# Attention queries kept once in fp32 and split on the chip before use, instead of stored and loaded as two parts

## The chip, the cores and the metric

One NeuronCore of a Trainium2 chip runs the whole program. The metric is the device time of one execution in microseconds (us); lower is better. Engines are named as the profile names them: PE (matrix multiply; PEld its weight loads), DVE (vector), ACT (scalar and activation), POOL and SP (here mainly issuers of DMAs).

## The reference

One layer of a hybrid encoder: a modulated RMSNorm, one input projection, a 2-D neighbourhood attention beside a bidirectional mLSTM, and one output projection with a residual and a final RMSNorm. Sequence 2048 (a grid of 32 rows by 64 columns), model width 1024, 8 attention heads of 64, all in fp32.

```python
proj = h @ w_in + b_in                       # (2048, 4624)
# attention: each token looks at 8 grid rows x 16 grid columns around it
qg = to_grid(q) * (NA_HEAD_DIM ** -0.5)
s = einsum('bhrcd,bhrjkd->bhrcjk', qg, kg) + bias[None]
s = where(col_mask[:, None, :], s, -inf)
p = softmax(s.reshape(..., kh * GRID_W), axis=-1)
o = einsum('bhrcjk,bhrjkd->bhrcd', p, vg)
na_out = o * silu(na_z)
# beside it: ml_out from a chunkwise bidirectional mLSTM
y = concatenate([na_out, ml_out], axis=-1) @ w_out
out = rmsnorm(x + gate * y)
```

## The kernel before

Products that need full accuracy are made as three fast passes: each operand is a high part (rounded to the fast matrix format, fp32r) and a low part (the rest), and high x high, low x high and high x low are summed in PSUM.

The program runs in stages. From 0 to about 520 us the norm, the token-side projections and the convolutions are made. Then `nq_gen` makes the remaining projections tile by tile as a generator (one `yield` per matmul, line 986), and `pump(n)` lets it run n matmuls between the steps of the mLSTM passes, so that PE always has something to do. For attention queries (kind `q`, 16 tiles of 128 channels x 512 tokens) ACT writes the high part from PSUM (line 1020), DVE the low part (line 1021), and both are stored to the DRAM scratch `d_qna`; the stores wait in the list `late` and are issued on ACT's queue a few matmuls later (line 989).

From about 960 us on, `phase2` runs the attention. The 16 patches of 128 queries have four units each (a unit is two heads), and two units are a pair. `slot(m)` works on pair m, and there are 32 slots with new scores. In a slot PE does, in this order: the 12 score matmuls of pair m (`scores`, line 1477, tile pS), the value matmuls of pair m-1 (line 1520, tile pO), a few matmuls of the output projection as filling (`pump`, line 1565, tile y), and then four times the transposes of one head's weights (`turned`, line 1505, tile pT), each followed by filling: 6, 5, 5, 4 and 4 matmuls in a steady slot, 8, 7, 7, 7 and 7 in the first three. The last four filling matmuls stand right before the scores of the next slot. DVE adds the bias table and takes the minimum (line 1485), ACT exponentiates (line 1486), DVE normalises (line 1497), and ACT copies each transposed tile out of PSUM (line 1507, tile pt). In every second slot, `mixed` also splits the patch's mixed heads for the output projection (ACT line 1535, DVE line 1540), while DVE adds finished output tiles to x (line 1570) and ACT squares them (line 1572).

The score matmuls of one unit take the query as their stationary operand, in pairs of heads: high query x high key, low query x high key, high query x low key. `load_q(m+2)`, at the start of slot m, loads a pair's queries, both parts at once, into one of three buffers `qs`; the first two go through POOL, the third through ACT, the others through SP. In slots 2 and 3 `split_w` splits the output weights (ACT line 1457, DVE line 1458, 128x1024 each).

Inside `manual_schedule` the instructions of an engine stand as the code emits them; outside, a scheduler places them. Everything from slot 0 on is emitted inside it; the end of the mLSTM before slot 0 is not.

Of the kernel before, what the change touches and what calls it, by code (L numbers as in the profile page):

```python
# [8 lines left out]
F32 = mybir.dt.float32  # L9
F32R = mybir.dt.float32r  # L10
AF = mybir.ActivationFunctionType
ALU = mybir.AluOpType
# [3 lines left out]
P = 128  # L16
# [4 lines left out]
GT = 512  # L21
# [41 lines left out]
class Kernel:  # L63
# [30 lines left out]
    def scratch(self):  # L94
        d = self.dram
        self.d_vna = d.tile([T, 512], F32, name="d_vna")
        self.d_ck = d.tile([MH, NC, P, 897], F32, name="d_ck")
        self.d_mneg = d.tile([P, CH], F32, name="d_mneg")
        self.d_zna = d.tile([16, P, 4, P], F32, name="d_zna")
        self.d_zml = d.tile([16, P, 4, P], F32, name="d_zml")  # L100
        self.d_qna = d.tile([2, 2, 16, P, 2, P], F32, name="d_qna")
        self.d_kna = d.tile([2, 512, T], F32, name="d_kna")
        self.d_mix = d.tile([16, P, 4, P], F32, name="d_mix")
        self.d_wo = d.tile([KT, P, D], F32, name="d_wo")
        self.d_fnw = d.tile([1, D], F32, name="d_fnw")
        self.d_gate = d.tile([1, D], F32, name="d_gate")
        self.d_rneg = d.tile([NH, 15, 31], F32, name="d_rneg")
        nks = [24, 32, 24]
        self.d_e = [d.tile([NH, 16, 15, nks[t]], F32, name=f"d_e{t}") for t in range(3)]
        nrs = [11, 15, 12]  # L110
        self.d_t = [[d.tile([NH, P, nrs[r] * nks[t]], F32, name=f"d_t{r}{t}") for t in range(3)] for r in range(3)]
# [853 lines left out]
    def nq_gen(self):  # L965
        nc = self.nc
        whi, wlo = self.wslot[0]
        both, upper, lower = range(NG), (3, 2), (1, 0)
        turns = [(s, both) for s in (0, 1, 2, 3)] + [(s, upper) for s in (4, 5, 6, 7, 8, 9, 10, 11, 12, 14, 13, 15)]
        turns += [(s, lower) for s in (8, 9, 10, 11, 4, 5, 6, 7)]  # L970
        turns += [(15, (1, 0)), (14, (1, 0)), (13, (1,)), (12, (1, 0)), (13, (0,))]
        order = [(i, s, g) for i, (s, gs) in enumerate(turns) for g in gs]
        needs = [i for i, (s, gs) in enumerate(turns) if i == 1 or i > 1 and s != turns[i - 2][0]]
        raw = self.nq_load(needs[0], turns[needs[0]][0])
        late, parity = [], False
        for i, s, g in order:
            off = (i % 2) * P
            kind, ct = ("mz", "nz", "k", "q")[s // 4], s % 4
            patch = kind != "k"
            col = {"mz": 20, "nz": 8, "k": 4, "q": 0}[kind] + ct  # L980
            bias = self.bcol[:, col : col + 1]
            ps = self.pp.tile([P, GT], F32, tag="pp", name=f"pq_{s}_{g}")
            for k in range(KT):
                w1, w2 = whi[:, k, off : off + P], wlo[:, k, off : off + P]
                for n, (w, h) in enumerate(((w1, self.hhi), (w1, self.hlo), (w2, self.hhi))):
                    self.mark = nc.tensor.matmul(patch_ps(ps) if patch else ps, w, self.htok(h, g, k, patch), start=(k == 0 and n == 0), stop=(k == KT - 1 and n == 2))  # L986
                    if k == 2 and n == 0:
                        while late:
                            nc.scalar.dma_start(*late.pop(0))
                    if i == len(turns) - 1 and k % 2 and n == 2:  # L990
                        self.lastload(k // 2)
                    if k == 2 and n == 0:
                        if needs and needs[0] == i + 1:
                            needs.pop(0)
                            self.nq_split(*raw)
                            if needs:
                                raw = self.nq_load(needs[0], turns[needs[0]][0])
                    if k < KT - 1 or n < 2:
                        yield
            if kind == "k" and g in lower:  # L1000

                hv, lv = (self.kk[ct][:, e * T + g * GT : e * T + (g + 1) * GT] for e in range(2))
                nc.scalar.activation(hv, ps, AF.Identity, bias=bias)
                nc.vector.scalar_tensor_tensor(lv, ps, bias, hv.bitcast(F32), ALU.add, ALU.subtract)
                yield
                continue
            parity = not parity
            if parity:
                both = self.qst.tile([P, 1032], F32R, tag="st", name=f"qst_{s}_{g}")
            else:  # L1010
                both = self.raw.tile([P, 1024], F32R, tag="raw1", name=f"qst_{s}_{g}")
            hv, lv = both[:, 0:512], both[:, 512:1024]
            if kind in ("mz", "nz"):
                hv = hv.bitcast(F32)
                nc.scalar.activation(hv, ps, AF.Silu, bias=bias)
                dst = (self.d_zna if kind == "nz" else self.d_zml)[4 * g : 4 * g + 4, :, ct].rearrange("a p q -> p a q")
                nc.scalar.dma_start(dst, hv.rearrange("p (a q) -> p a q", a=4))
                self.zdone.add((kind, ct, g))
            else:
                nc.scalar.activation(hv, ps, AF.Identity, bias=bias)  # L1020
                nc.vector.scalar_tensor_tensor(lv, ps, bias, hv.bitcast(F32), ALU.add, ALU.subtract)
                for e, part in enumerate((hv, lv)):
                    src = part.bitcast(F32).rearrange("p (a q) -> p a q", a=4)
                    if kind == "q":
                        dst = self.d_qna[e, ct // 2, 4 * g : 4 * g + 4, :, ct % 2].rearrange("a p q -> p a q")
                    else:
                        dst = self.d_kna[e, ct * P : (ct + 1) * P, g * GT : (g + 1) * GT].rearrange("p (a q) -> p a q", a=4)
                    late.append((dst, src))
            if (s, g) in ((15, 3), (15, 2)):
                self.freed.append(g)  # L1030
            yield
        while late:
            nc.scalar.dma_start(*late.pop(0))
# [308 lines left out]
    def phase2(self):  # L1342
        nc = self.nc
# [44 lines left out]
        def load_q(i):  # L1388
            if 2 * i >= NU:
                return  # L1390
            b, c0 = units[2 * i][0], min(units[2 * i][1], units[2 * i + 1][1])
            (nc.gpsimd, nc.gpsimd, nc.scalar, nc.sync)[min(i, 3)].dma_start(qs[i % 3].bitcast(F32), self.d_qna[:, c0 // 2, b].rearrange("e p c q -> p e c q"))

        def load_v(b, most=4, queue=nc.gpsimd):

# [285 lines left out]
        def slot(m):  # L1681
            new = (2 * m, 2 * m + 1) if 2 * m < NU else ()
            old = (2 * m - 2, 2 * m - 1) if m else ()
            if m:
                load_q(m + 2)
            if new:
                scores(new)
            if old:
                po = values(old)
            if new:  # L1690
                normalised(new[0])
            if old:
                gated(old, po)
            if new:
                normalised(new[1])
            b = units[old[0]][0] if m > 2 and old[0] % 4 == 2 else None
            if not new:
                mixed(b, 1)
                mixed(b, 0)
                for _ in range(2):  # L1700
                    self.pump(12)
                    finish()
                    step()
                return
            fills = [8, 7, 7, 7, 7] if m < 3 else [6, 5, 5, 4, 4]
            for n in range(-1, 4):
                if n >= 0:
                    turned(new[n // 2], n % 2)
                    if n % 2:
                        step()  # L1710
                    finish()
                    if n in (1, 2) and b is not None:
                        mixed(b, n % 2)
                    if n in (0, 2):
                        loads(new[n // 2])
                    if n == 1 and self.reloads:
                        self.reloads.pop(0)()
                for fn in extra.pop((m, n), ()):
                    fn()
                self.pump(fills[n + 1])  # L1720
            if m == 2:
                self.pump(max(0, self.left) + 1)
                self.owed = 0
                mixed(b0, 1)
                mixed(b0, 0)

        with self.tc.manual_schedule():
            for m in range(NU // 2 + 1):
                slot(m)
            while len(done) < len(patches):  # L1730
# [85 lines left out]
```

## Time and profile before

| | |
|---|---|
| median of 3 runs | 1331.33 us (1327.65 to 1332.96) |
| profiled execution, its own time | 1328.63 us |
| its span | 1326.9 us |
| PE busy | 1294.6 us, 98% |
| DVE, ACT, POOL busy | 779.6 us (59%), 542.8 us (41%), 225.1 us (17%) |
| DMA | 255.91 MB, mean 193 GB/s |

The span runs from the first to the last instruction of the program; the execution's own time has 1.7 us around it. A row of the timeline has start, duration, engine, line, operation and tiles, and in brackets how long the engine was idle before and who ended it. Names such as hhi, hlo, whi_a are those of buffers that are used again: in the score matmuls `hhi` and `hlo` hold attention keys, in the output projection the weights.

### The profile page before, as it was taken

To read this page: it belongs to the slowest core of one execution; us is meant where nothing else is said; L and a number is where in the kernel's file an instruction comes from. 1 tells how busy PE (TensorE), PEld (TensorE's weight loads), DVE (VectorE), ACT (ScalarE), POOL (GpSimd) and SP (SyncE) were. 2 spreads that over 40 slices of the span, in tenths; PEclk is the share of its full clock that TensorE was granted. 3 is DMA by queue.
4 is the path that set the end of the run, shared out by engine and by line. 5 is a ranking of instruction groups with operands and counts; after the bars stand their busy time and mean duration, and the time that the engine had idled before them with its cause. 6 is when DMAs were issued, how large, how long until landed. Compare 5 with 4: busy or idle time off the path is not lost. (4 is left out here: it accounts for less than half of the span.)

```text
span 1326.9 us, 23404 instructions
## 1 busy us (share of the span) xinstructions
PE 1294.6 (98%) x8330; PEld 1115.4 (84%) x8330; DVE 779.6 (59%) x2406; ACT 542.8 (41%) x1184; POOL 225.1 (17%) x280
## 2 busy tenths in 40 slices
PE   9999999999999999999999999999999999999996
PEld 8899999999878787888888888888777778778785
DVE  5754452112455559176768878767547576666663
ACT  5643324543222323123324323333356555565551
POOL 0243103331000000012212002121202211212211
PEclk9999999999999999999999999999999999999999
DMA  9998657998267685545756866746689977868871
GB/s 325 323 281 180 169 141 171 214 244 217 82 149 208 142 209 165 159 120 167 204 165 196 254 187 204 237 141 188 198 256 239 212 184 190 195 175 194 195 186 48
DMA packets 240487, 255.91 MB, mean 193 GB/s; under 512 B 31079, under 2 KB 200295, under 8 KB 240371
## 3 DMA queue, kind: packets, MB, share of 16 engines
q1 hardware_dynamic: 157006, 182.98, 50.7%
q0 software_dynamic: 20496, 36.21, 11.2%
q10 hardware_dynamic: 62868, 35.22, 9.6%
q8 instruction: 66, 1.08, 0.4%
q14 instruction: 51, 0.41, 0.1%
HBM read 169.81 MB, written 92.72 MB: 198 GB/s over the span
## 5 line engine op out<-in xcount | busy, mean ns | idle before, releaser
L986 PE MATMUL pq<-hhi,whi_a 128*128 128x512 f32 x512 | 208.2, 407 | 0.8 <-ACT u L891 0.8
L986 PE MATMUL pq<-hlo,whi_a 128*128 128x512 f32 x512 | 208.4, 407 | 0.0
L986 PE MATMUL pq<-hhi,wlo_a 128*128 128x512 f32 x512 | 206.7, 404 | 0.0
L986 PEld LDWEIGHTS pq<-hhi,whi_a 128*128 128x128 f32 x512 | 96.8, 189 | 17.8 <-ACT u L891 1.3
L986 PEld LDWEIGHTS pq<-hhi,wlo_a 128*128 128x128 f32 x512 | 96.8, 189 | 16.3
L986 PEld LDWEIGHTS pq<-hlo,whi_a 128*128 128x128 f32 x512 | 96.7, 189 | 16.0 <-issue 0.5
L1507 ACT ACTIVATE pt<-pT 96x384 f32<-96x384 f32 (+3 forms) x128 | 65.8, 514 | 86.7 <-PE pT L1505 84.0
L1486 ACT ACTIVATE pbuf<-pbuf,mn 128x480 f32<-128x480 f32 (+5 forms) x128 | 76.0, 594 | 53.0 <-DVE mn L1485 53.0
L960 POOL TENSOR_TENSOR wlo_a<-rawq,whi_a 128x1024 fp32r<-128x1024 f32 x19 | 45.8, 2409 | 296.1 <-ACT whi_a L959 263.7
L1565 PE MATMUL y<-hhi,whi_a 128*128 128x512 f32 x256 | 91.4, 419 | 0.5 <-ACT whi_a L1535 0.5
L1565 PE MATMUL y<-hhi,wlo_a 128*128 128x512 f32 (+1 forms) x272 | 90.7, 399 | 0.2 <-ACT y L1572 0.2
L1485 DVE CUSTOM_DVE_ANT_0 pbuf<-pS,tab 128x480 f32<-128x480 f32 (+5 forms) x128 | 62.9, 540 | 39.1 <-PE pS L1477 32.1
L1230 ACT ACTIVATE num<-px,gtile 128x129 f32<-128x129 f32 x120 | 38.3, 366 | 111.3 <-PE px L1225 86.5
L1505 PEld LDWEIGHTS pT<-ident,pbuf 128*128 128x128 f32 (+2 forms) x416 | 51.0, 137 | 29.6 <-issue 9.9
L618 DVE TENSOR_TENSOR stvo<-pvo,brow 128x256 f32<-128x256 f32 x64 | 26.6, 422 | 83.1 <-PE pvo L548 65.7
L1505 PE MATMUL pT<-ident,pbuf 128*128 128x128 f32 (+2 forms) x416 | 67.3, 275 | 8.2 <-DVE pbuf L1497 6.8
L546 PE MATMUL pvo<-whi_b,hhi 128*128 128x256 f32 x256 | 72.6, 284 | 0.0
L548 PE MATMUL pvo<-whi_b,hlo 128*128 128x256 f32 x256 | 72.1, 281 | 0.0
L547 PE MATMUL pvo<-wlo_b,hhi 128*128 128x256 f32 x256 | 72.0, 281 | 0.0
L1249 POOL TENSOR_TENSOR hm<-hm,ck 128x128 f32<-128x128 f32 x64 | 26.5, 414 | 252.9 <-DVE hm L1248 223.9
L833 ACT ACTIVATE dec<-dec,gtile 128x128 f32<-128x128 f32 x128 | 42.7, 393 | 53.6 <-POOL dec L826 50.8
L581 DVE TENSOR_TENSOR stv<-pv,brow 128x256 f32<-128x256 f32 x32 | 12.4, 421 | 74.4 <-DMA d_vna<-stv 43.4
(302 smaller groups left out, 3408.3 us busy)
## 6 DMA issues: line engine op xcount, KB each, us to landing
ck<-d_ck SPq DMA_DIRECT2D x64, 384.5 KB
rawq<-in_w_main_dram SPq DMA_DIRECT2D x28, 512.0 KB
raw<-in_w_main_dram SPq DMA_DIRECT2D x20, 512.0 KB
d_ck<-stvo SPq DMA_DIRECT2D x16, 514.0 KB
kv<-d_ck SPq DMA_DIRECT2D x64, 128.5 KB
wada<-in_w_ada_dram SPq DMA_DIRECT2D x32, 256.0 KB
dec<-d_mneg SPq DMA_DIRECT2D x32, 256.0 KB
d_ck<-dec ACTq DMA_DIRECT2D x32, 256.0 KB
```

Source lines behind the costliest of these rows:

```text
L546: nc.tensor.matmul(ps, lhi(k), rhi(k), start=(k == 0), stop=False)
L547: nc.tensor.matmul(ps, lhi(k), rlo(k), start=False, stop=False)
L548: self.mark = nc.tensor.matmul(ps, llo(k), rhi(k), start=False, stop=(k == KT - 1))
L833: nc.scalar.activation(t[:, o, :], t[:, o, :], AF.Exp, bias=self.cols["g"][:, d, h, c : c + 1])
L960: (eng or nc.gpsimd).tensor_tensor(lo[:, :, cs], raw, hi[:, :, cs].bitcast(F32), ALU.subtract)
L986: self.mark = nc.tensor.matmul(patch_ps(ps) if patch else ps, w, self.htok(h, g, k, patch), start=(k == 0 and n == 0), stop=(k == KT - 1 a ...
L1230: nc.scalar.activation(num[:, d, :], px[:, d, :], AF.Copy, scale=self.cols["inter"][:, d, h, c : c + 1])
L1485: nc.vector.tensor_tensor_reduce(pt[:, :nk], ps, tabs[place[u]][j][:, :nk], 1.0, 3e38, ALU.add, ALU.min, mn)
L1486: nc.scalar.activation(pt[:, :nk], pt[:, :nk], AF.Exp, bias=mn, scale=-1.0, accum_out=sums[:, j : j + 1])
L1505: nc.tensor.transpose(ps[:cs, i, :], U[u][j][:, i * cs : (i + 1) * cs], self.ident)
L1507: nc.scalar.activation(t[:cs, :nch, :], ps[:cs, :nch, :], AF.Copy)
L1565: nc.tensor.matmul(y, m[:, k, :], w[k][:, cs], start=(k == 4 and n == 0), stop=(k == 3 and n == 2))
```

## The change

Queries are stored once, in fp32: ACT alone evicts the tile, and one store leaves instead of two. `load_q` loads that single copy into the low half of the buffer. The new `split_q(i)` makes the parts on the chip: ACT copies the loaded values, rounded, into the high half, and DVE subtracts the high half from the low half in place. `slot(m)` calls `split_q(m + 1)` after its fourth transposes and before its last four filling matmuls; `split_q(0)` is called before slot 0.

```diff
-        self.d_qna = d.tile([2, 2, 16, P, 2, P], F32, name="d_qna")
+        self.d_qna = d.tile([2, 16, P, 2, P], F32, name="d_qna")
...
+            elif kind == "q":
+                hv = hv.bitcast(F32)
+                nc.scalar.activation(hv, ps, AF.Identity, bias=bias)
+                dst = self.d_qna[ct // 2, 4 * g : 4 * g + 4, :, ct % 2].rearrange("a p q -> p a q")
+                late.append((dst, hv.rearrange("p (a q) -> p a q", a=4)))
             else:
                 nc.scalar.activation(hv, ps, AF.Identity, bias=bias)
                 nc.vector.scalar_tensor_tensor(lv, ps, bias, hv.bitcast(F32), ALU.add, ALU.subtract)
...
-            (nc.gpsimd, nc.gpsimd, nc.scalar, nc.sync)[min(i, 3)].dma_start(qs[i % 3].bitcast(F32), self.d_qna[:, c0 // 2, b].rearrange("e p c q -> p e c q"))
+            (nc.gpsimd, nc.gpsimd, nc.scalar, nc.sync)[min(i, 3)].dma_start(qs[i % 3][:, 1].bitcast(F32), self.d_qna[c0 // 2, b])
+
+        def split_q(i):
+            if 2 * i < NU:
+                hi, lo = qs[i % 3][:, 0], qs[i % 3][:, 1]
+                nc.scalar.activation(hi, lo.bitcast(F32), AF.Copy)
+                nc.vector.tensor_tensor(lo, lo.bitcast(F32), hi.bitcast(F32), ALU.subtract)
...
+                if n == 3:
+                    split_q(m + 1)
                 self.pump(fills[n + 1])
...
         with self.tc.manual_schedule():
+            split_q(0)
             for m in range(NU // 2 + 1):
                 slot(m)
```

The order of ACT's instructions at the end of slot 18 and the start of slot 19, a slot with mixing, before (pt is the copy of a transposed tile, y the square, pbuf the exponential of the next slot's scores):

```order
L1572 ACTIVATE y_0_12389,fss_12387<-xr_12428 128x512
L1535 ACTIVATE whi_a<-zs 128x512
L1507 ACTIVATE pt_1_12568<-pT_1_12563 128x512
L1486 ACTIVATE pbuf_10151,sums_12592<-pbuf_10151,mn_0_12593 128x480
L1486 ACTIVATE pbuf_10152,sums_12592<-pbuf_10152,mn_1_12596 128x480
```

and in the changed kernel:

```order
L1580 ACTIVATE y_0_12393,fss_12391<-xr_12432 128x512
L1543 ACTIVATE whi_a<-zs 128x512
L1515 ACTIVATE pt_1_12574<-pT_1_12569 128x512
L1399 ACTIVATE qs_10029<-qs_10029 128x256
L1494 ACTIVATE pbuf_10133,sums_12600<-pbuf_10133,mn_0_12601 128x480
```

The high part of slot 19's queries is made behind the last copy of slot 18's transposed tiles, and nothing else moved. DVE at the same place, before (whi_a is the low part of the mixed heads, xr the sum with x):

```order
L1540 TENSOR_TENSOR whi_a<-whi_a 128x512
L1570 TENSOR_TENSOR xr_12428<-xr_12428,y_0_12389 128x512
L1540 TENSOR_TENSOR whi_a<-zs,whi_a 128x512
L1570 TENSOR_TENSOR xr_12428<-xr_12428,y_1_12431 128x512
L1485 ISA pbuf_10151,mn_0_12593<-pS_0_12576,tab_10051 128x480
```

and in the changed kernel:

```order
L1548 TENSOR_TENSOR whi_a<-whi_a 128x512
L1578 TENSOR_TENSOR xr_12432<-xr_12432,y_0_12393 128x512
L1548 TENSOR_TENSOR whi_a<-zs,whi_a 128x512
L1400 TENSOR_TENSOR qs_10029<-qs_10029 128x256
L1578 TENSOR_TENSOR xr_12432<-xr_12432,y_1_12435 128x512
L1493 ISA pbuf_10133,mn_0_12601<-pS_0_12584,tab_10035 128x480
```

The low part stands behind the mixed heads' low part. The third place is DVE before slot 0, outside the hand-written order, where the last mLSTM group is normalised (an iterated root, nwt and rstd, then mu). In the changed kernel:

```order
L1339 TENSOR_TENSOR nwt_3_10012<-rstd_3_10009 128x4
L1637 MEMSET pbuf_10135 128x512
L1340 SCALAR_TENSOR_TENSOR nwt_3_10012<-nwt_3_10012,var_3_10008 128x4
L1400 TENSOR_TENSOR qs_10028<-qs_10028 128x256
L1341 SCALAR_TENSOR_TENSOR rstd_3_10009<-nwt_3_10012,rstd_3_10009 128x4
L1339 TENSOR_TENSOR nwt_3_10012<-rstd_3_10009 128x4
L1340 SCALAR_TENSOR_TENSOR nwt_3_10012<-nwt_3_10012,var_3_10008 128x4
L1341 SCALAR_TENSOR_TENSOR rstd_3_10009<-nwt_3_10012,rstd_3_10009 128x4
L1264 SCALAR_TENSOR_TENSOR mu_3_10022<-mv_3_9847,rstd_3_10009 128x4
```

There the scheduler set the first low part in the middle of that root; before, the same rows stand there without it. On ACT the first high part stands ahead of the four activations that use mu. On PE the first transpose that needs those activations (ht, line 1282) stands two filling matmuls later than before.

More of the change, by code (lines that the diff above doesn't have):

```diff
@@ L1023, in nq_gen @@
                     src = part.bitcast(F32).rearrange("p (a q) -> p a q", a=4)
[L1024 to L1027, printed above, removed]
+                    dst = self.d_kna[e, ct * P : (ct + 1) * P, g * GT : (g + 1) * GT].rearrange("p (a q) -> p a q", a=4)
                     late.append((dst, src))
```

## The prediction

> **What bounds the kernel now.** I read the page first, then the busy time of the attention's steady stretch, then who PE waits for.
>
> ```profile
> span 1326.9 us, 23404 instructions
> PE 1294.6 (98%) x8330; PEld 1115.4 (84%) x8330; DVE 779.6 (59%) x2406; ACT 542.8 (41%) x1184; POOL 225.1 (17%) x280
> ...
> 1045.00:1290.00 245.00, 240.25 (x1800) 190.42 (x1801) 160.70 (x525) 135.16 (x349) 46.60 (x74) 1.00 0.78 192
> ...
> PE pT L1505 <- DVE pbuf L1497: 4.7, 4, 2.0
> ```
>
> The third row gives, for 1045 to 1290 us, the busy time of PE, PEld, DVE, ACT and POOL, then the granted clock and the DMA share. PE is busy for 240 of 245 us, at full clock. The last row is all that PE waits for in that stretch: 4.7 us, four times, for normalised weights. PE takes its instructions in order and has no slack, so a new wait of PE lengthens the program by its own length, unless it falls ahead of one of these four; work taken off DVE, ACT or the queues shortens nothing. So the question is whether the new split is ready when the scores want it.
>
> **What the change takes away.** Queries need one store instead of two, one load of half the size, and no low part at eviction: 16 of these 24 DVE instructions go, 16 x 0.746 = 12 us of DVE. Nobody on PE is waiting for them. PE's waits while the queries are made (750 to 960 us) are these:
>
> ```profile
> L1021 DVE SCALAR_TENSOR_TENSOR qst<-pq,bcol,qst x24: 735/746/751, 697.9 to 997.9; 128x512 fp32r<-128x512 f32 x24
> ...
> PE ht L1282 <- ACT hm L1274: 1.5, 2, 1.2
> PE px L1225 <- DVE st L1149: 0.7, 1, 0.7
> PE a L1212 <- DMA ck<-d_ck: 0.4, 1, 0.4
> ...
> 1150.26 0.42 SPq L1392 DMA_DIRECT2D qs<-d_qna  x1
> ```
>
> The waits add up to 2.6 us, and their releasers are the mLSTM's own chains, so the gain lies between 0 and 2.6 us; I take 0. The loads stay early: the one in the last row fills the buffer for slot 20, and slot 18 starts only at 1156.
>
> **What the split costs in a slot.** The high part is one ACT copy of 128x256, the low part one DVE subtraction of 128x256, which waits for it. The shapes nearest to them:
>
> ```profile
> L1535 ACT ACTIVATE whi_a<-zs 128x512 fp32r<-128x512 f32 x8 | 4.9, 615 | 0.0
> L1457 ACT ACTIVATE hhi<-hlo 128x1024 fp32r<-128x1024 f32 x8 | 8.4, 1052 | 0.0
> L1527 DVE TENSOR_TENSOR zs<-pO,zs 128x256 f32<-128x256 f32 x16 | 6.6, 414 | 0.0
> L1477 PEld LDWEIGHTS pS<-hlo,qs 64*128 64x128 f32 x190 | 15.5, 184 | 6.4 <-issue 3.7 <-DMA tab<-d_t 2.2
> ```
>
> Each is a group with its busy time and mean ns. The copy goes from 1052 ns to 615 for half the columns, so a quarter takes 615 - 437/2 = 0.40 us; the subtraction takes 0.42.
>
> Where does it stand? The name "a pair ahead" suggests a whole slot of cover, but the order in the code puts both instructions behind the last copy of the slot's transposed tiles, and between those transposes and the next scores PE has only four filling matmuls. At the start of slot 18, at 1156 us, after a slot without mixing:
>
> ```profile
> 1155.39 0.49 ACT L1507 ACTIVATE pt<-pT 128x384 f32<-128x384 f32 x1 [0.77 <-PE pT L1505]
> 1155.58 0.39 PE L1565 MATMUL y<-hlo,wlo_a 128*128 128x512 f32 x1
> ...
> 1155.81 0.40 PE L1565 MATMUL y<-hhi,wlo_a 128*128 128x512 f32 x1
> 1156.14 0.94 PE L1477 MATMUL pS<-hlo,qs 64*128 64x480 f32 x6
> ...
> 1157.67 1.53 PE L1520 MATMUL pO<-pt,v 128*64 128x128 f32 x24
> ```
>
> and of slot 19, at 1166.7 us, after a slot with mixing:
>
> ```profile
> 1166.03 0.62 ACT L1535 ACTIVATE whi_a<-zs 128x512 fp32r<-128x512 f32 x1
> ...
> 1166.55 0.58 ACT L1507 ACTIVATE pt<-pT 128x512 f32<-128x512 f32 x1
> 1166.67 0.69 DVE L1540 TENSOR_TENSOR whi_a<-zs,whi_a 128x512 fp32r<-128x512 f32 x1 [1.31 <-ACT whi_a L1535]
> 1166.68 0.94 PE L1477 MATMUL pS<-hlo,qs 64*128 64x480 f32 x6
> ```
>
> From these rows: filling matmuls follow one another in 0.23 us; twelve score matmuls, six pairs, take 1157.67 - 1156.14 = 1.53 us, so the second pair, the first that needs the low part, starts 0.26 after the first; ACT starts its next instruction 0.10 before the end of the last (1166.65 against 1166.55); DVE starts 0.02 after ACT's end (1166.67). For the step from DVE to PE I take 0.10.
>
> Slot 18: ACT could copy at 1155.88 - 0.10 = 1155.78, done 1156.18; DVE 1156.20 to 1156.62; PE 1156.72, against 1156.40 before: 0.32 us late. The late pair's weights must then be loaded with nothing to hide behind, between 0 and the 0.18 of the weight load above; I take 0.08, together 0.40.
>
> Slot 19: the last copy ends at 1167.13, the high part at 1167.43. DVE is on the mixed heads' low part until 1167.36, then subtracts 1167.45 to 1167.87; PE 1167.97 against 1166.94: 1.03, with the weight load 1.11. Behind the waiting ACT and DVE instructions stand only the exponentials and the x sum, which PE does not want sooner.
>
> Slots 6 to 31 are of these two kinds, 13 each: 13 x 0.40 + 13 x 1.11 = **19.6 us**. Slots 1 and 2 have seven filling matmuls there, 3 x 0.23 = 0.69 us more cover, and no mixing: 0. Four of the late slots run into the waits for normalised weights of the first fence (4.7 us together), where later scores only shorten that wait: between 4 x 0.40 = 1.6 and 4 x 1.11 = 4.4 us come back; I take the middle, **-3.0 us**.
>
> **Slots 3 to 5 and the start.** Rows of ACT, DVE and PE:
>
> ```profile
> 996.55 0.76 PE L1477 MATMUL pS<-hhi,qs 64*128 64x360 f32 x6
> ...
> 996.66 0.69 ACT L1020 ACTIVATE qst<-pq,bcol 128x512 fp32r<-128x512 f32 x1
> 996.73 1.23 DVE L1458 TENSOR_TENSOR hlo<-hlo,hhi 128x1024 fp32r<-128x1024 f32 x1 [0.73 <-ACT hhi L1457]
> ...
> 999.06 0.63 ACT L1535 ACTIVATE whi_a<-m 128x512 fp32r<-128x512 f32 x1 [1.71 <-DVE qst L1021]
> ...
> 999.74 0.50 PE L1565 MATMUL y<-hhi,whi_a 128*128 128x512 f32 x1 [0.48 <-ACT whi_a L1535]
> ...
> 1003.55 0.87 PE L1505 MATMUL pT<-ident,pbuf 128*120 128x128 f32 x3 [1.88 <-DVE pbuf L1497]
> ...
> 1010.04 2.58 DVE L1458 TENSOR_TENSOR hlo<-hlo,hhi 128x1024 fp32r<-128x1024 f32 x2 [0.25 <-ACT hhi L1457]
> ...
> 1010.63 0.76 PE L1477 MATMUL pS<-hlo,qs 64*128 64x360 f32 x6
> ...
> 1020.75 0.76 PE L1477 MATMUL pS<-hlo,qs 64*128 64x360 f32 x6
> ...
> 1021.11 0.60 ACT L1572 ACTIVATE y<-xr 128x512 f32<-128x512 f32 x1 [0.63 <-DMA xr<-in_x_dram]
> ```
>
> Slot 3: the low part stands behind a weight split that ends at 997.96, so the second pair goes at 998.5 instead of 996.8, 1.7 us late. But PE already waits 0.48 + 1.88 us behind it, because ACT's mixing waits for the last query's low part (999.06). That part goes: ACT makes the copy (0.40), evicts the last query tile (0.69, from 996.66 on), issues one store (about 0.5, an estimate from the issue in the row of SP above) and mixes at about 998.2, 0.86 earlier, and the transpose at 1003.55 comes earlier with it. Net **-0.9**. Slot 4: weight splits to 1012.62, then 0.42: the pair due at 1010.9 goes at 1013.1: **+2.2**. Slot 5: the square ends at 1021.71, copy and subtraction at 1022.5, due 1021.0: **+1.6**.
>
> The first split is different, since ACT and DVE now wait for a DMA in the middle of the last mLSTM group:
>
> ```profile
> 937.81 0.93 POOL L1392 DMA_DIRECT2D qs<-d_qna  x1 [0.31 <-POOL hm L1249]
> ...
> DMA to landing us min/median/max: 5.8/6.1/6.3
> ...
> 942.00 0.10 DVE L1338 SCALAR_TENSOR_TENSOR nwt<-nwt,var 128x4 f32<-128x4 f32 x1
> ...
> 942.93 0.16 DVE L1262 SCALAR_TENSOR_TENSOR mu<-mv,rstd 128x4 f32<-128x4 f32 x1
> ...
> 943.73 0.33 PE L1282 MATMUL ht<-perm,hm 128*128 128x128 f32 x1 [0.30 <-ACT hm L1274]
> ```
>
> The load lands 6.1 us after its issue, at about 944.0; 0.40 + 0.42 later, at 944.8, the root goes on; it takes 0.99 (942.10 to 943.09), and PE's transpose comes 0.64 after that: 946.4 instead of 943.73. Two filling matmuls more, 0.46, stand ahead of it now: **+2.2 us**, between 0 (half the bytes land sooner) and 3.
>
> **The sum.** 19.6 - 3.0 - 0.9 + 2.2 + 1.6 + 2.2 = 21.7. On the profiled execution's own 1328.63 that gives 1350.3; its time is 2.7 below the runs' median of 1331.33, from which it would be 1353.0. I take **1352**, between the two.
>
> **Rivals.** *The waits cool the clock.* What a PE wait does to the clock is seen twice (same columns as above):
>
> ```profile
> 1003.40:1006.80 3.40, 3.25 (x11) 2.68 (x12) 2.33 (x7) 1.96 (x4) 0.00 (x0) 0.50 1.02 357
> ...
> 1148.00:1152.00 4.00, 1.99 (x11) 1.38 (x10) 3.17 (x12) 2.30 (x7) 0.00 (x0) 1.00 0.99 206
> ```
>
> After the 1.88 us wait the clock was 0.50 for 3.4 us, which costs 1.7 us of work; a wait of 2.0 in the second stretch left it at 1.00. If each of the 13 longer waits did this, 13 x 1.7 = 22 us more: 1374. For it: the first row. Against it: the second, and that 1.1 us is well under 1.88. The Trainium skill, "TensorE: Matmul & The Clock Gate", HAM oscillation, asks only that PE gaps stay under about 3.4 us, by which none of these waits would cool the clock and the sum would stay; the first row disagrees with it. Chance 0.07.
>
> *Not slower: the cover is enough.* If copy and subtraction were through within 0.26 us of the first score matmul, at the cost of ACT's and DVE's idle time alone, the 19.6 us go; and if the halved loads bring the bias tables sooner, the 4.7 us of table waits go too: 1328.6 - 4.7 = 1324. It decides at 0.4 us in slots without mixing and 1.1 in the others, by which the chain would have to be shorter than 0.82 us of execution. For it: DVE and ACT are far from full. Against it: both are in order, and the split stands behind the last copy. Chance 0.06, half of it with the table waits unchanged, within 0.5%.
>
> *Only the mixing slots pay.* If PE's queue hides up to 0.4 us, 5.2 us go: about 1346, inside the range.
>
> **How the numbers follow.** Forecast 0.87, the third rival among it. Its range: at the low end the steady slots cost 0.15 and 0.85 us (13.0 in all), 3.0 come back, the start costs nothing and slots 3 to 5 half of their 2.9: 1328.6 + 11.4 = 1340. At the high end they cost 0.6 and 1.3 (24.7), 1.6 come back, the start costs 3, slots 3 to 5 all, and two stretches of cool clock 3.4: 32.4 on the median, 1364, rounded to 1365. The range 1340 to 1365 leaves out the two outer rivals, 0.13, and little else. A measurement of this kernel can tell about 0.5% (6.7 us) from no change: slower 0.92, same 0.05, faster 0.03.
>
> **What would show it.** Right: a wait of PE at the score matmuls (line 1485 of the changed kernel) for the DVE subtraction of qs, near 0.3 us in slots after no mixing, near 1.0 after mixing; DVE busy about the same (12 us off, 32 x 0.42 = 13 on), ACT some 13 us more; 4.2 MB less stored and 4.2 MB less loaded; one wait of 2 to 3 us at ht near 944. Wrong: scores that start without a wait, a copy or subtraction far from 0.4 us, ACT's copy ahead of the last pt, or a clock of 0.50 in many slots.

## The result, and the profile after

The changed kernel takes 1350.1 us (median of 4 runs, 1348.52 to 1350.41) against 1331.96 (4 runs, 1327.65 to 1332.96): ratio 1.0143, 95% interval 1.012 to 1.0165, so it is slower by 16 to 22 us. The forecast was 1352. The first rows of the page:

```profile
span 1348.3 us, 23448 instructions
PE 1306.3 (97%) x8330; PEld 1119.4 (83%) x8330; DVE 785.4 (58%) x2422; ACT 553.8 (41%) x1216; POOL 226.4 (17%) x280
...
DMA packets 228134, 247.52 MB, mean 184 GB/s; under 512 B 30822, under 2 KB 188006, under 8 KB 228018
```

The span is 21.4 us longer. DMA moves 255.91 - 247.52 = 8.4 MB less, PE executes as many matmuls as before, and ACT and DVE stay far from full. Nothing in these rows says why the kernel is slower. The waits of PE from 800 us to the end do (columns: us in total, times, longest):

```profile
PE pS L1485 <- ACT qs L1399: 12.9, 17, 1.4
PE pT L1513 <- DVE pbuf L1505: 2.2, 1, 2.2
PE pS L1485 <- DVE qs L1400: 1.7, 2, 0.9
```

The first and third rows are new: score matmuls that wait for the split. They add up to 14.6 us, and not to 20, for two reasons. The wait for the low part comes between two score matmuls, where the profile counts part of it as PE busy (six score matmuls show as 1.17 us instead of 0.94 in the rows below), and short waits are not listed. So I measured each slot from its last filling matmul to the first value matmul, in both traces; that stretch holds the same matmuls in both.

Slot 18, after a slot without mixing:

```profile
1167.46 0.49 ACT L1515 ACTIVATE pt<-pT 128x384 f32<-128x384 f32 x1 [0.78 <-PE pT L1513]
1167.85 0.41 ACT L1399 ACTIVATE qs<-qs 128x256 fp32r<-128x256 f32 x1
1167.90 0.39 PE L1573 MATMUL y<-hhi,wlo_a 128*128 128x512 f32 x1
1168.29 0.43 DVE L1400 TENSOR_TENSOR qs<-qs 128x256 fp32r<-128x256 f32 x1 [2.54 <-ACT qs L1399]
1168.31 1.17 PE L1485 MATMUL pS<-hlo,qs 64*128 64x480 f32 x6
1170.08 1.53 PE L1528 MATMUL pO<-pt,v 128*64 128x128 f32 x24
```

From the last filling matmul (1167.90) to the value matmuls (1170.08) it is 2.18 us; before, 1157.67 - 1155.81 = 1.86. The ACT copy stands directly behind the last copy of pt, the subtraction follows it, and the scores start 0.05 after the copy's end at 1168.26. Slot 19, after a slot with mixing:

```profile
1176.22 0.60 PE L1513 MATMUL pT<-ident,pbuf 128*128 128x128 f32 x4
...
1178.94 0.58 ACT L1515 ACTIVATE pt<-pT 128x512 f32<-128x512 f32 x1
1179.07 0.69 DVE L1548 TENSOR_TENSOR whi_a<-zs,whi_a 128x512 fp32r<-128x512 f32 x1 [1.31 <-ACT whi_a L1543]
1179.42 0.40 ACT L1399 ACTIVATE qs<-qs 128x256 fp32r<-128x256 f32 x1
1179.86 0.42 DVE L1400 TENSOR_TENSOR qs<-qs 128x256 fp32r<-128x256 f32 x1
1179.88 1.17 PE L1485 MATMUL pS<-hlo,qs 64*128 64x480 f32 x6 [0.72 <-ACT qs L1399]
1180.33 0.30 PEld L1485 LDWEIGHTS pS<-hlo,qs 64*128 64x128 f32 x4 [0.27 <-DVE qs L1400]
```

The first row is slot 18's third set of transposes, which comes back below. Here ACT's copy ends at 1179.82 and PE, which has stood for 0.72 us, goes on at 1179.88. Then the weight load of the second pair waits until the subtraction ends at 1180.28.

### The profile page after: what moved, and what is told of

Read it like the earlier page. It is cut to its first block, busy times and chain, and to the rows that moved or that the text cites. A ratio compares the mean times of both kernels' runs of the same rounds, so it can differ in the third digit from the quotient of the medians.

```text
span 1348.3 us, 23448 instructions
## 1 busy us (share of the span) xinstructions
PE 1306.3 (97%) x8330; PEld 1119.4 (83%) x8330; DVE 785.4 (58%) x2422; ACT 553.8 (41%) x1216; POOL 226.4 (17%) x280
## 2 busy tenths in 40 slices
DMA packets 228134, 247.52 MB, mean 184 GB/s; under 512 B 30822, under 2 KB 188006, under 8 KB 228018
## 4 chain that ended last, share of the span: by engine, by line
PE 82%; DMA 6%; ACT 4%; DVE 4%; issue 2%; SPq 0%; ACTq 0%; POOL 0%; DVEq 0%; POOLq 0%
PE pq L986 24%; PE y L1573 9%; PE pc L546 4%; PE pc L547 4%; PE pc L548 4%; PE pvo L546 3%; PE pvo L548 3%; PE pvo L547 3%; PE pO L1528 3%; PE pvo L601 3%; PE pS L1485 3%; PE pT L1513 3%; PE pv L548 2%; PE pv L547 2%; PE pv L546 2%
## 5 line engine op out<-in xcount | busy, mean ns | idle before, releaser
L1573 PEld LDWEIGHTS y<-hhi,wlo_a 128*128 128x128 f32 x272 | 48.6, 191 | 9.0 <-issue 2.4
```

The lines of the kernel that those rows point to most:

```text
L1573: nc.tensor.matmul(y, m[:, k, :], w[k][:, cs], start=(k == 4 and n == 0), stop=(k == 3 and n == 2))
```

## The experiments

Boundary cost is what the stretch from last filling to first value matmul is longer than before, as a mean over the 13 slots after slots without mixing and the 13 after slots with mixing (slots 6 to 31). The last column is the profiled span from the start of slot 0 to the end, because the stretch ahead of slot 0 differs by up to 7 us from one profiled execution to the next, also where kernels don't differ there. It also holds stretches of 3.4 us at half clock, 1.7 us of lost work each, that differ between executions: from slot 0 to the tail before has one, after two, e1 and e5 none, the others one each. Each ratio is to runs of before made beside that kernel; their medians are 1331.96, 1333.04 (e1 to e4) and 1333.32 (e5 to e7).

| kernel | median us | ratio to before (95%) | boundary, no mixing | boundary, mixing | slot 0 to end |
|---|---|---|---|---|---|
| before | 1331.96 | | | | 367.4 |
| after | 1350.10 | 1.0143 (1.012 to 1.0165) | 0.43 | 1.11 | 388.7 |
| e1_split_early | 1329.74 | 0.9977 (0.9954 to 1.0) | 0.00 | 0.00 | 363.6 |
| e2_idle_split | 1335.63 | 1.0017 (0.9992 to 1.0041) | 0.00 | 0.00 | 372.2 |
| e3_low_last | 1342.92 | 1.0073 (1.0052 to 1.0095) | 0.25 | 0.94 | 381.5 |
| e4_split_n2 | 1343.63 | 1.0069 (1.0047 to 1.009) | 0.00 | 1.00 | 379.3 |
| e5_double_load | 1331.42 | 0.9983 (0.9966 to 1.0001) | 0.00 | 0.00 | 365.6 |
| e6_split_early_again | 1329.46 | 0.9973 (0.9954 to 0.9992) | 0.00 | 0.00 | 366.0 |
| e7_more_fill_last | 1338.83 | 1.0039 (1.002 to 1.0059) | 0.00 | 0.64 | 374.7 |

**The split, earlier in the slot.** The theory is that the place behind the last transposes costs the time; the first rival is that splitting on the chip costs it wherever it stands.

```diff
-                if n == 3:
+                if n == 0:
                     split_q(m + 1)
```

> The changed kernel with its split moved to after the first transposes of the slot ahead (n == 0 instead of n == 3), about 5 us sooner. If only the late place costs (theory): no wait of PE for the parts of qs, the 20 us of slots 6 to 31 and the 5.5 us of slots 3 to 5 go, time 1328 to 1333 us, no more than 0.3% from the kernel before. If ACT's and DVE's added work costs wherever it stands (rival): at least 1342 us. If the halved queries' traffic also ends waits for the bias tables (rival): under 1325 us.

PE's waits from 950 us on:

```profile
PE pT L1513 <- DVE pbuf L1505: 4.3, 8, 1.4
```

No score matmul waits for a split. The same 32 copies and 32 subtractions cost nothing that can be seen when they stand three transposes earlier: the slowdown, 16 to 22 us, is the place. That the halved loads hide a cost of the split is unlikely: with loads of the old size (e5, below) the early split is not slower than before either.

**The split's work alone.** Here the kernel before keeps its two loads; from slot 3 on, a copy and a subtraction of the same size are added at the place that the changed kernel uses. They write to a buffer that nobody reads.

```diff
+        def split_spare(i):
+            if i > 3 and 2 * i < NU:
+                hi, lo = m0[:, 0:2], m0[:, 2:4]
+                nc.scalar.activation(hi, qs[i % 3][:, 1].bitcast(F32), AF.Copy)
+                nc.vector.tensor_tensor(lo, qs[i % 3][:, 1].bitcast(F32), hi, ALU.subtract)
...
+                if n == 3:
+                    split_spare(m + 1)
```

> The kernel before, queries stored and loaded in two parts, with a copy and a subtraction of the same size added at the changed kernel's place (from slot 3 on), written to a spare buffer that nobody reads. Theory (PE pays only for waiting on the parts): within 3 us of the kernel before. Rival (25 us more work on ACT and DVE delays exponentials and normalisation): 10 us or more slower, with longer waits of PE at the transposes.

It adds 2.6 us by the medians, with an interval that holds no change and up to 5.5 us. The scores start without a wait. The largest of PE's waits from 950 us on is the one for normalised weights, as in the kernel before, where it is 6.8 us in six:

```profile
PE pT L1511 <- DVE pbuf L1503: 9.5, 8, 2.1
```

So ACT's and DVE's time at that place is nearly free, even at the worst place; it is PE's dependence on the result that costs.

**The low part wanted last.** The score passes run as high x high, high query x low key, low query x high key. The low part is wanted one pair later, by the 0.26 us between pairs; the high part is wanted when it was.

```diff
-                for n, (e, f) in enumerate(((0, 0), (1, 0), (0, 1))):
+                for n, (e, f) in enumerate(((0, 0), (0, 1), (1, 0))):
```

> The changed kernel with the pair of score matmuls that takes the low query put last of three. Theory: the wait for the high part stays (about 0.1 us after slots without mixing, 0.84 after mixing), the second wait of 0.13 to 0.24 us for the low part goes: 26 x 0.18 us and about 0.5 us in slots 3 and 4, time about 1345 us. Rival (the low part alone decides): the waits of 0.4 and 1.1 us shrink by a whole pair, 0.26 us or more each, under 1342 us. Rival (PE only restarts late, order does not matter): 1350 us.

The waits are nearly all for the high part:

```profile
PE pS L1485 <- ACT qs L1399: 13.0, 17, 1.3
PE pS L1485 <- DVE qs L1400: 1.4, 2, 0.7
```

The boundary cost falls by 0.18 and 0.17 us a slot, 26 slots: 20.0 - 15.4 = 4.6 us. That is what the low part's place in the order is worth. Of the rest, 0.25 and 0.94, the first score matmul's wait for the high part is 0.14 and 0.82, which reordering doesn't touch; 0.11 stays behind it, and no experiment separates that. From slot 0 to the end it is 388.7 - 381.5 = 7.2 us; the remaining 2.6 are about what slot 17 cost more in the changed kernel (below): its wait for normalised weights is 1.3 us here instead of 2.2, and no half clock follows it.

**One transpose earlier.** The split after the third transposes instead of the fourth.

```diff
-                if n == 3:
+                if n == 2:
                     split_q(m + 1)
```

> The changed kernel with its split one step earlier (n == 2): ahead of the last copy of transposed tiles on ACT, but behind the mixing on ACT and DVE. Theory (ACT's and DVE's order decides): after slots without mixing no wait; after mixing slots the subtraction still stands behind the mixed heads' low part, so about 1.0 us stays: 13 x 0.43 + 13 x 0.1, about 7 us less, 1343 us. Rival (matmuls of cover decide: four filling matmuls and the transposes more, about 1.2 us): both waits go, 1330 us.

After slots without mixing nothing is left; after mixing it is still 1.00. Slot 19 of this kernel shows why:

```profile
1170.32 0.40 ACT L1399 ACTIVATE qs<-qs 128x256 fp32r<-128x256 f32 x1
1170.44 0.69 DVE L1548 TENSOR_TENSOR whi_a<-zs,whi_a 128x512 fp32r<-128x512 f32 x1 [1.31 <-ACT whi_a L1543]
1170.62 0.57 ACT L1515 ACTIVATE pt<-pT 128x512 f32<-128x512 f32 x1
1170.77 0.49 PE L1485 MATMUL pS<-hlo,qs 64*128 64x480 f32 x2 [0.23 <-ACT qs L1399]
1171.05 0.42 DVE L1400 TENSOR_TENSOR qs<-qs 128x256 fp32r<-128x256 f32 x1
1171.53 0.71 PE L1485 MATMUL pS<-hlo,qs 64*128 64x480 f32 x4 [0.27 <-DVE qs L1400]
```

The copy now stands ahead of the last pt, but behind the mixing on ACT; the subtraction still queues behind the mixed heads' low part on DVE, starts 0.33 us after the copy has ended, and the second pair follows it. PE's waits are split evenly:

```profile
PE pS L1485 <- DVE qs L1400: 4.7, 14, 0.6
PE pS L1485 <- ACT qs L1399: 4.6, 13, 0.4
```

So the two kinds of slot have two causes: without mixing, the place behind the last pt; with mixing, also the queue behind the mixed heads' split on both engines. The next kernel tries the same from the other side.

**More filling behind the split.** Three filling matmuls are moved from ahead of the split to behind it; their number stays 24.

```diff
-            fills = [8, 7, 7, 7, 7] if m < 3 else [6, 5, 5, 4, 4]
+            fills = [8, 7, 7, 7, 7] if m < 3 else [5, 4, 4, 4, 7]
```

> The changed kernel, split at its late place, with the same filling dealt out as 5, 4, 4, 4 and 7 matmuls instead of 6, 5, 5, 4 and 4, so that three more (0.69 us) cover the split. Theory (cover decides): no wait after slots without mixing, about 0.4 us after mixing, 14.6 us less at the scores; but transposes come closer together and wait up to 0.2 us each for the tile copied out before, so 1336 to 1342 us. Rival (the split's execution itself costs): 1348 us or more.

PE's three largest waits from 950 us on (in total), and the end of slot 18 with the start of slot 19:

```profile
PE pS L1485 <- ACT qs L1399: 4.9, 15, 0.7
PE y L1573 <- ACT y L1580: 1.9, 1, 1.9
PE pS L1485 <- DVE qs L1400: 1.7, 2, 0.9
```

```profile
1170.33 0.65 PE L1513 MATMUL pT<-ident,pbuf 128*128 128x128 f32 x4
...
1172.14 0.60 ACT L1580 ACTIVATE y<-xr 128x512 f32<-128x512 f32 x1 [0.47 <-DVE xr L1578]
...
1172.77 0.62 ACT L1543 ACTIVATE whi_a<-zs 128x512 fp32r<-128x512 f32 x1
1173.29 0.58 ACT L1515 ACTIVATE pt<-pT 128x512 f32<-128x512 f32 x1
...
1173.77 0.40 ACT L1399 ACTIVATE qs<-qs 128x256 fp32r<-128x256 f32 x1
```

Three filling matmuls, 0.69 us, take away the 0.43 entirely, but only 0.47 of the 1.11, where the theory had about 0.4 left. The rows show the rest. After mixing, ACT reaches the last pt not when the transposes are done but when it has squared an output tile, for which it waits for DVE, and has mixed. From the third transposes to the high part it is 1173.77 - 1170.33 = 3.44 us here and 1179.42 - 1176.22 = 3.20 in the changed kernel: this chain doesn't shorten with PE's work ahead of it, and 0.69 - 0.24 = 0.45 is what the three matmuls bring. The closer transposes, which I expected to wait, cost nothing that shows: the boundary cost is 11.8 us less than in the changed kernel over slots 6 to 31 and 2.0 less in slots 3 to 5, and from slot 0 to the end 388.7 - 374.7 = 14.0 are gone. The second row is new: a filling matmul in slot 5 waits for a squared tile, and a half clock follows, together 3.5 us; the changed kernel's wait and half clock at slot 17 are as long, so the two about cancel in this difference.

**The loads.** e1 halves the bytes of each query load. To see whether that pays, e5 is e1 with each load bringing the fp32 queries twice.

```diff
-            ...dma_start(qs[i % 3][:, 1].bitcast(F32), self.d_qna[c0 // 2, b])
+            ...dma_start(qs[i % 3].bitcast(F32), self.d_qna[c0 // 2, b].unsqueeze(1).broadcast_to([P, 2, 2, P]))
```

> The first experiment's kernel (split early), but each load brings the fp32 queries twice, into both halves, so that the loads are as large as before the change (the stores stay halved). Theory (the loads are off PE's path but for the first one): the load lands in about 5.4 us instead of 3.5, the first split and the mLSTM's last transposes (ht) wait about 2 us more, otherwise nothing: 0 to 3 us above the first experiment. Rival (less traffic is what the early split gains by): waits for the bias tables come back, 4 us or more above it.

> The first experiment's kernel again, in more rounds, as the version that may beat both: theory (no split wait, one late query part less ahead of the first mixing): 2 to 4 us under the kernel before, 0.997 to 0.9985 of it. Rival (its 0.23% was noise): 1.000 within 0.1%.

```profile
DMA to landing us min/median/max: 4.1/4.4/4.7
...
PE ht L1284 <- ACT hm L1276: 1.3, 1, 1.3
```

These rows are of e5; the landing was expected at 5.4. In the same kernel with single loads, run beside it, the wait at ht is 0.5.

Doubling adds 2.0 us by the medians, but the two intervals overlap, and from slot 0 to the end it shows nothing (365.6 against 366.0 and 363.6 for the same kernel twice). The waits for normalised weights between 1045 and 1292 us do differ: 4.7 us before, 2.7 and 3.2 with the early split and single loads, 4.4 with doubled ones. So the rival may be part of it, but well under its 4 us, and these are single executions: what the halved loads are worth, between nothing and a few us, stays open. The early split is faster than the kernel before by a little, 0.9973 (0.9954 to 0.9992), where its first series, 0.9977, had left no change just inside the interval. Part of this gain can be placed: in both profiled executions of this kernel slot 3 is 2.75 us shorter than before. Mixing no longer waits for the last query's low part (0.5 us), the wait for normalised weights is 1.4 instead of 1.9, and no half clock follows it (1.7).

## Why the prediction was right, point by point

**Steady slots: 19.6 predicted, 20.0 measured.** The steps hold: 0.40 forecast and 0.43 measured without mixing, 1.11 and 1.11 with it. So do the durations:

```profile
L1399 ACT ACTIVATE qs<-qs x32: 399/404/417, 941.8 to 1309.1; 128x256 fp32r<-128x256 f32 x32
L1400 DVE TENSOR_TENSOR qs<-qs x32: 418/425/427, 942.3 to 1309.5; 128x256 fp32r<-128x256 f32 x32
...
DMA to landing us min/median/max: 3.7/3.8/3.8
```

One reading was off without changing the sum: I expected the wait to be shown at the DVE subtraction. The first pair already waits for ACT's high part: it starts 0.07 to 0.36 us later than before without mixing (mean 0.14), 0.78 to 0.86 with it (0.83). The stretch behind its start is 0.23 to 0.34 longer in both kinds (0.28). That the copy itself is late I had seen, but I had priced only the later of the two ends; after mixing the earlier one carries most. The 0.10 from DVE's end to PE's start had no row; slot 19 shows 0.05 (1180.28 to 1180.33).

**Waits for normalised weights: 3.0 predicted to come back, about 1.6 measured.** Of the four of before (4.7 us) three went, 2.7 us together. One is this row of before,

```profile
PE pT L1505 <- DVE pbuf L1497: 1.6, 1, 1.6
```

the other two are of 0.5 and 0.6 us. The step "I take the middle" treated them alike; the fourth, 2.0 us in slot 17, stayed, at 2.2, although the scores of that slot started 10 us later than before. The term took the tables' landing as fixed in time. Their loads are issued from within the slots and so come later with them (the third of slot 16 goes 3.9 us after that slot's start in both kernels), and DVE still waits for one in slot 17, 1.6 us before and 2.0 in the changed kernel:

```profile
1157.80 0.56 DVE L1493 CUSTOM_DVE_ANT_0 pbuf<-pS,tab 128x384 f32<-128x384 f32 x1 [1.99 <-DMA tab<-d_t]
```

Why the other three went is not shown. Behind the wait of slot 17 the clock halved:

```profile
1011.90:1015.30 3.40, 3.40 (x27) 2.93 (x26) 2.90 (x13) 2.42 (x8) 2.25 (x4) 0.50 0.54 141
1162.10:1165.50 3.40, 3.40 (x11) 2.70 (x10) 2.98 (x12) 0.52 (x2) 0.00 (x0) 0.50 0.56 194
1180.00:1183.40 3.40, 3.40 (x44) 2.65 (x44) 3.20 (x11) 1.62 (x5) 1.19 (x2) 1.00 0.47 124
```

3.4 us at a clock of 0.50 (third column from the end) is 1.7 us of work lost: -2.7 + 0.2 + 1.7 = -0.8, and 0.8 more came back in small pieces that I have not traced. Whether such a wait halves the clock was a matter of where it fell (last section), so this 1.7 is chance.

**Slots 3 to 5: 2.9 predicted, 2.5 measured.** The scores wait 1.6, 2.2 and 1.7 us, and slot 3's mixing comes earlier, as forecast. The half clock of slot 3 is gone, which the forecast had left out: slot 3, from the last filling matmul ahead of it to its own last, is 2.5 us shorter where 0.9 was forecast. But one appears in slot 4 (first row above), and that slot is 3.3 us longer where 2.2 was forecast. That the two clock effects cancel in the sum is luck. The new one stands behind these two waits, the first 0.97 and the second 0.86 us:

```profile
1009.66 0.43 PE L1485 MATMUL pS<-hlo,qs 64*128 64x360 f32 x2 [0.97 <-ACT qs L1399]
1010.95 0.60 PE L1485 MATMUL pS<-hlo,qs 64*128 64x360 f32 x4 [0.86 <-DVE qs L1400]
```

**The start: 2.2 predicted, 0.5 measured** (slot 0 starts 0.17 us later than before and is 0.33 longer). This term was mis-sized. The step that failed is "the load lands 6.1 us after its issue": the load is half as large now and lands after 3.8 (the row above).

```profile
937.95 0.78 POOL L1394 DMA_DIRECT2D qs<-d_qna  x1 [0.31 <-POOL hm L1251]
...
941.81 0.42 ACT L1399 ACTIVATE qs<-qs 128x256 fp32r<-128x256 f32 x1 [1.43 <-issue]
942.26 0.42 DVE L1400 TENSOR_TENSOR qs<-qs 128x256 fp32r<-128x256 f32 x1
943.38 0.16 DVE L1264 SCALAR_TENSOR_TENSOR mu<-mv,rstd 128x4 f32<-128x4 f32 x1
944.12 0.33 PE L1284 MATMUL ht<-perm,hm 128*128 128x128 f32 x1 [0.33 <-ACT hm L1276]
```

DVE reaches its subtraction when the data is there, mu comes 0.45 us later than before, and PE's wait at ht is 0.33 instead of 0.30. I had held that as the lower bound, "half the bytes land sooner", but took a value near the upper one from the large load's row. In e5, where the first load lands after 4.7, the same wait is 1.3. The wait itself grew by only 0.03; how much of the 0.5 is the split's stays open, because the start of slot 0 varies by more than that from one profiled execution to the next.

**The sum:** 0.5 + 2.5 + 20.0 - 1.6 = 21.4, the difference of the spans. Forecast were 21.7. The steady slots, by far the largest term, were forecast by their mechanism; that the total comes within 0.3 is luck, since two smaller terms are off by about 1.5 each, in opposite directions. The profile of before was of one of its shorter executions; between the medians it is 18.1.

**The rivals.** *The waits cool the clock* did not happen in the steady slots: the third windows row above, 0.1 us behind the wait of slot 19, is at 1.00, and none of the 13 longer waits was followed by half clock. It did happen behind 2.2 us and behind 0.97 + 0.86 us, a matter of PE's idle time within 3.4 us (last section). The Trainium skill, "TensorE: Matmul & The Clock Gate", HAM oscillation, asks for PE gaps under about 3.4 us; by it none of these would cool the clock. The rows disagree for the gap of 2.2 us and agree for the single ones of about 1. *The cover is enough* is what e1 makes true, at 1329.7 rather than 1324: the waits for normalised weights between 1045 and 1292 us, 4.7 before, then are 2.7, less but not gone. *Only the mixing slots pay* is false in the changed kernel (0.43 in the other slots) and true in e4.

## What to carry to other kernels

"A pair ahead" says little: what covers a new producer is the work that the consumer's engine still has between the producer's place in its own in-order queue and the use, here four matmuls (0.9 us) against a copy and a subtraction of 0.40 and 0.42 us that start only behind the last copy of pt. Count that from the rows at the place, for each kind of slot, because an instruction of another job ahead of it in either queue (here the mixed heads' split) counts in full. The same work put where both engines are ahead of need cost nothing that shows, and that kernel as a whole is 0.1 to 0.5% faster than before.

## What the runs showed of the hardware that was not expected

- The first two query loads land 5.8 to 6.3 us after their issue with both parts (before) and 5.3 to 5.6 (e2), after 3.2 to 3.9 with half the bytes (the six profiles with single loads), and after 4.1 to 4.7 with the half brought twice (e5). So size alone does not set it: 256 KB that bring 128 KB twice land sooner than 256 KB of two parts. What else does was not tried.
- PE's clock goes to 0.50 for 3.41 us at a time, and its changes stand on a grid: in each trace the times at which the granted clock changes lie whole multiples of 3.413 us apart (1003.38 - 40.82 = 962.56 = 282 x 3.413 in before, 1162.11 - 1011.92 = 150.19 = 44 x 3.413 in after). Between slot 0 and 1310 us of all nine profiles, each of the eight stretches of this grid in which PE was busy for at most 1.72 us of the 3.41 was followed by one at half clock, and none in which it was busy for 1.75 or more. One stretch of before, then two of after (the second number is PE's busy time):

```profile
1146.74:1150.15 3.41, 1.79 (x10) 1.05 (x6) 1.78 (x8) 1.52 (x6) 0.00 (x0) 1.00 0.94 257
...
1008.51:1011.92 3.41, 1.58 (x13) 0.98 (x12) 2.62 (x4) 1.10 (x2) 0.00 (x0) 1.00 0.53 142
1158.69:1162.11 3.42, 1.20 (x8) 0.98 (x8) 2.63 (x11) 2.86 (x9) 0.00 (x0) 1.00 0.98 198
```

  The 2.0 us wait of before ends at 1150.54, across the grid's line at 1150.15, and the clock stays; the 2.2 us of after lie within one stretch, and it halves. Ahead of slot 0 the bound is less sharp: 1.50 us busy at 450.4 in before was not followed by half clock. No run was made to test this.
- The stretch ahead of slot 0 varies between profiled executions: slot 0 starts at 959.4 us in before and at 959.6 to 966.4 in the others. Differences of a few us between two spans must be read from slot 0 on, or from medians.
